# Reversing the column order of the single-pass matmuls in a hybrid decoder block

## The chip, the cores and the metric

The kernel runs on one core of a Trainium2 chip. The metric is device time in microseconds, the median of several runs of the whole program. A profile of one execution gives each instruction of the core's engines: TensorE (PE, and PEld for its weight loads), VectorE (DVE), ScalarE (ACT), GpSimd (POOL), and SyncE (SP), which issues DMA transfers.

## The reference

One layer of a decoder block over 512 tokens of width 1024, in float32:

```python
h = rms_norm(x, norm_mix_pre)
proj = h @ w_in                      # q, k, v, gates of both mixers
o_gla = gla_mixer(...)               # chunked gated linear attention, 4 heads
o_nsa = nsa_mixer(...)               # compressed + selected + window attention, 8 heads
mixed = (sigmoid(merge_gla) * (o_gla @ w_proj_gla)
         + sigmoid(merge_nsa) * (o_nsa @ w_proj_nsa))
x = x + rms_norm(mixed @ w_out, norm_mix_post)
h = rms_norm(x, norm_ffn_pre)
f = (silu(h @ w_ffn_gate) * (h @ w_ffn_up)) @ w_ffn_down     # inner width 2816
x = x + rms_norm(f, norm_ffn_post)
```

Nearly all of the arithmetic is in the dense products with weights.

## The kernel before

A matmul on TensorE loads a weight tile of up to 128 x 128 (the stationary operand) and then streams the columns of a moving operand past it; the results, column by column, go to one bank of PSUM (128 partitions x 512 float32 columns), where they replace what is there or are added to it.

**Single-pass products.** Float32 operands that need full precision are split into two tiles of type float32r, a rounded high part and the rest: `xh`, `xl` for activations, `wh`, `wl` for weights. A product is then three matmuls that add up in PSUM: `wh` with `xh`, `wh` with `xl`, `wl` with `xh`. A float32r matmul reads its columns once, and is called single-pass here. The others work on plain float32 and have two records each in the profile: the transposes with `ident`, the inner products of the linear attention (L585 to L636), the compression (L836) and the compressed scores (L886).

**Where the single-pass products are**, in the order of the program:

- the token-major part of `w_in` (L463 to L465): 3 groups of 440 columns, over 4 token blocks and 8 blocks of the model width;
- `prod` (L174 to L176), used by `dense_h` and others: 128 output features by all 512 tokens (or half of them), over the model width in steps of 128;
- `eproduct` (L383): pairs of weight tiles of `w_in` in a seven-product scheme on halves (256 columns), with sums of activations and weights formed beforehand (`EF`, `eform`);
- the gates of the linear attention (L519), 512 columns;
- the attention: scores (`part` in `scores`, L970 and L971, widths 128 to 512), the start of a head (L1010) and the weighted values (`add` in `values`, L1034 to L1037, widths 512 down to 128);
- `ffn_half` (L1258 to L1260): the first feed-forward blocks, 256 columns;
- `product` in `unit` (L1416): 19 feed-forward blocks in the same seven-product scheme, 256 columns, 84 matmuls each;
- `down_product` (L1706): the down projection in that scheme, 256 columns, 147 matmuls per pair of output blocks.

All their operands have columns that lie next to each other in memory. Among the float32 matmuls, `compress` reads its moving operand with a step of 16 floats:

```python
blocks = ct.rearrange("p b (n s) -> p b n s", s=16)
pe.matmul(ps[:, 0:130].rearrange("p (b n) -> p b n", b=2), cw1[:, p, :], blocks[:, :, o:o + 65, w], ...)
```

**Order of the work.** The tile framework takes the instructions in the order in which the kernel's code issues them to the five engines (with a few marked to be issued after others) and puts semaphores where a tile is written by one engine and read by another. `Stream` loads weights on SP's queue some tiles ahead; ScalarE makes the high part, and VectorE, or an adding DMA of POOL's queue, the low part. PSUM has four tags of two banks each (`mm`, `sc`, `tp`, `acc`); VectorE and ScalarE read a bank when the last matmul of its group has ended.

Of the kernel before, what the change touches and what calls it, by code (L numbers as in the profile page):

```python
# [18 lines left out]
KD = D // 128  # L19
# [73 lines left out]
def hybrid_block_kernel(ctx: ExitStack, tc: tile.TileContext, I, outT):  # L93
# [4 lines left out]
    wts = ctx.enter_context(tc.tile_pool(name="wts", bufs=1, side="right"))  # L98
    psum = ctx.enter_context(tc.tile_pool(name="psum", bufs=1, space=PSUM))

    def bank(tag):
        return psum.tile([128, 512], F32, tag=tag, bufs=2, name="ps_" + tag)

# [63 lines left out]
    def prod(ps, w, xh, xl, k0, kn, ktot, t=ALL):  # L167

        wh, wl = w
        marks = []  # L170
        for kk in range(kn):
            k = k0 + kk
            c = slice(kk * 128, (kk + 1) * 128)
            pe.matmul(ps[:, t], wh[:, c], xh(k)[:, t], start=(k == 0), stop=False)  # L174
            pe.matmul(ps[:, t], wh[:, c], xl(k)[:, t], start=False, stop=False)  # L175
            marks.append(pe.matmul(ps[:, t], wl[:, c], xh(k)[:, t], start=False, stop=(k == ktot - 1)))  # L176
        return marks

    def hh(k):
# [188 lines left out]
    def eproduct(u, i):  # L368
        a, b = USE[i]
        if a == "a11":  # L370
            p = [bank("mm"), bank("mm")]
            ebank[u] = p if u % 2 == 0 else p[::-1]
            eus[u] = gt.tile([128, 2, 256], F32, tag="eus", bufs=1, name="eus")
        p1, p2 = ebank[u]
        r1, rb, r2, ra = p1[:, 0:256], p1[:, 256:512], p2[:, 0:256], p2[:, 256:512]
        u2, u3 = eus[u][:, 0, :], eus[u][:, 1, :]
        o, first = {"a11": (r1, True), "s2": (r2, True), "s3": (rb, False), "s1": (ra, False), "a12": (r1, False),
                    "a22": (rb, False), "s4": (ra, False)}[a]
        (wh, wl), (xh, xl) = ew.pop((u, a)), EF[b]
        for q in range(4):  # L380
            c = slice(q * 128, (q + 1) * 128)
            for m, (w, x) in enumerate(((wh, xh), (wh, xl), (wl, xh))):
                pe.matmul(o, w[:, c], x[q], start=(first and q == 0 and m == 0), stop=(q == 3 and m == 2),  # L383
                          skip_group_check=True)

        def add(out, y):
            return dve.tensor_tensor(out=out, in0=o, in1=y, op=OP.add)  # L387

        if a == "a11":
            out_of[u, a] = act.copy(u2, o)  # L390
        elif a == "s2":
            add(u2, u2)
        elif a == "s3":
            out_of[u, a] = add(u3, u2)
        else:
            if u not in edst:
                edst[u] = [early_dest(n) for n in EPAIRS[u]]
            d0, d1 = edst[u]
            if a == "s1":
                add(d1[:, halves[1]], u3)  # L400
            elif a == "a22":
                add(d1[:, halves[0]], u2)
            elif a == "s4":
                out_of[u] = add(d0[:, halves[1]], u2)
            else:
                act.copy(d0[:, halves[0]], o)
                for n in EPAIRS[u]:
                    if T_R <= n < T_MA:
                        proj_r(n - T_R)
# [40 lines left out]
    for g in range(3):  # L450
        pss = [bank(t) for t in tags[g]]
        for c in range(4):
            wh, wl = st.next(("tok", g, c))
            for i in range(NT):
                if (g, c, i) == (0, 3, 2):
                    ps = token_sums([acc_x], "acc")
                    rsqrt_mean(rs_x, ps[:, 0:NT], D, EPS)
                t = slice(i * 128, (i + 1) * 128)
                for kk in range(2):
                    k = 2 * c + kk  # L460
                    w = slice(kk * TG, (kk + 1) * TG)
                    o = pss[i][:, 0:TG]
                    pe.matmul(o, hu[:, k, t], wh[:, w], start=(k == 0), stop=False)  # L463
                    pe.matmul(o, hul[:, k, t], wh[:, w], start=False, stop=False)
                    pe.matmul(o, hu[:, k, t], wl[:, w], start=False, stop=(k == KD - 1))  # L465
            if g > 0:
                beside.pop(0)()
        if g == 0:
            ps = over_partitions(rs_x, "acc")
            act.copy(rb_x, ps)  # L470
        for i in range(NT):
            c0, c1 = g * TG, (g + 1) * TG
            if c0 < 1024:
                act.activation(out=tok[i][:, c0:min(c1, 1024)], in_=pss[i][:, 0:min(c1, 1024) - c0], func=AF.Copy,
                               scale=rs_x[:, i:i + 1])
            if c1 > 1024:
                act.activation(out=tokb[:, i, 0:c1 - 1024], in_=pss[i][:, 1024 - c0:TG], func=AF.Copy,
                               scale=rs_x[:, i:i + 1])
# [34 lines left out]
    def gates_two(h0):  # L513
        aT, w3 = stk["a"], stk["w"]
        for h in (h0, h0 + 1):
            low = gt.tile([128, S], F32, tag=("e2", "dd", "sr", "sr")[h],
                          bufs=(1, 2, 4, 4)[h], name="low")
            ps = bank("sc")
            pe.matmul(ps, w3[:, h * 128:(h + 1) * 128], aT, start=True, stop=True)  # L519
            stk["abs"] = act.activation(out=lam[:, h], in_=ps, func=AF.Abs, bias=b_alpha[:, h:h + 1])  # L520
            dve.tensor_scalar(out=low, in0=ps, scalar1=b_alpha[:, h:h + 1], scalar2=0.0,
                              op0=OP.add, op1=OP.min)
            lows.append(low)
# [431 lines left out]
    def scores(h, b):  # L955
# [7 lines left out]
        def part(blks, last):  # L963
            ps = bank("sc")
            col = 0
            for i in blks:
                n = 128 * (i + 1)
                s = ps[:, col:col + n]
                t = slice(i * 128, (i + 1) * 128)
                pe.matmul(s, q1[:, t], ka[b][:, 0:n], start=True, stop=False)  # L970
                pe.matmul(s, q3[0:66, t], kb[b][0:66, 0:n], start=False, stop=True)  # L971
                col += n
            col = 0
            for i in blks:
                n = 128 * (i + 1)
                s = ps[:, col:col + n]
                o = p[:, OFF[i]:OFF[i] + n]
                dve.tensor_tensor_reduce(out=o, in0=s, in1=causal[:, S - n:S], scale=-1.0, scalar=-NEG,  # L978
                                         op0=OP.add, op1=OP.min, accum_out=mx[:, i:i + 1])
                act.activation(out=o, in_=o, func=AF.Exp, scale=-1.0, bias=mx[:, i:i + 1],  # L980
                               accum_out=z[:, i:i + 1])
                col += n
            if last:
                dve.reciprocal(z, z)
                dve.tensor_tensor(out=z, in0=z, in1=gates[:, :, 3 * h + (1 if b == "s" else 2)], op=OP.mult)
                for i in range(NT):
                    n = 128 * (i + 1)
                    o = p[:, OFF[i]:OFF[i] + n]
                    dve.tensor_scalar(out=o, in0=o, scalar1=z[:, i:i + 1], scalar2=None, op0=OP.mult)  # L989
# [17 lines left out]
    def head_start(h):  # L1007
        ps = bank("acc")
        accs[h] = ps
        pe.matmul(ps, vc3[:, h // 4, :], c3s.pop(h), start=True, stop=False)  # L1010

    def values(h, b):
        p = units.pop((h, b))
# [15 lines left out]
        def add(k):  # L1029
# [1 line left out]
            r = slice(k * 128, S)  # L1031
            end = b == "w" and k == NT - 1
            if not end:
                pe.matmul(ps[:, r], vv[b][:, k, :], ph[:, r], start=False, stop=False)  # L1034
            pe.matmul(ps[0:64, r], vv[b][:, k, 0:64], pl[:, r], start=False, stop=False)
            if end:
                pe.matmul(ps[:, r], vv[b][:, k, :], ph[:, r], start=False, stop=True)  # L1037

        return turn, add

# [207 lines left out]
    def ffn_half(e, w, ps, ks=range(KD)):  # L1248
# [3 lines left out]
        for k in ks:  # L1252
            i, j = k // 2, k % 2
            c = slice(k * 128, (k + 1) * 128)
            for x in range(2):
                wh, wl = w[x]
                o = ps[x][:, t]
                pe.matmul(o, wh[:, c], h2h[i][:, j, t], start=(k == 0), stop=False)  # L1258
                pe.matmul(o, wh[:, c], h2l[i][:, j, t], start=False, stop=False)
                last = pe.matmul(o, wl[:, c], h2h[i][:, j, t], start=False, stop=(k == KD - 1))  # L1260
            marks.append(last)
        return marks

# [141 lines left out]
    def unit(n, between=None):  # L1405
# [5 lines left out]
        def product(o, a, b, first):  # L1411
            (ah_, al_), (bh_, bl_) = forms.pop((n, a)), XF[b]
            for q in range(4):
                c = slice(q * 128, (q + 1) * 128)
                for i, (w, x) in enumerate(((ah_, bh_), (ah_, bl_), (al_, bh_))):
                    pe.matmul(o, w[:, c], x[q], start=(first and q == 0 and i == 0), stop=(q == 3 and i == 2),  # L1416
                              skip_group_check=True)

        def add(out, ps, b):
# [269 lines left out]
    def down_product(j):  # L1689
# [13 lines left out]
        for q in range(KH):  # L1703
            c = slice(q * 128, (q + 1) * 128)
            for i, (w, x) in enumerate(((wh, xh), (wh, xl), (wl, xh))):
                pe.matmul(o, w[:, c], x[q], start=(first and q == 0 and i == 0), stop=(q == KH - 1 and i == 2),  # L1706
                          skip_group_check=True)
        if a == "a11":
            act.copy(u2, r1)
# [143 lines left out]
```

## Time and profile before

| | |
|---|---|
| median of 3 runs | 864.79 us (864.34 to 865.26) |
| span of the profiled execution, first to last instruction | 862.0 us (its time as a run is not listed apart from the span) |
| mean granted TensorE clock | 0.996 |
| TensorE busy | 845.4 us, 98% |
| weight loads busy | 769.0 us, 89% |
| VectorE, ScalarE, GpSimd busy | 635.0, 530.2, 141.4 us |
| TensorE's share of the chain that ended last | 85% |

Matmuls are pipelined and their ends are modelled: a matmul's row is longer than the distance to the next one's start. The time of a stream of matmuls is therefore read from starts, or from the chain, in which each piece begins where the one before ended. A group of instructions is a line of the kernel with its engine, operation, tiles (out<-in) and shape; behind the bar stand its busy time, the mean of one in ns, and the idle time before. An instruction inside a helper has the helper's line.

### The profile page before, as it was taken

The page shows a single profiled execution, that of the slowest core. Times are in us where ns is not written, and L with a number is a line of the kernel's source. Part 1 is how long each engine was busy: PE and PEld are TensorE (multiplying, and loading weights), DVE is VectorE, ACT ScalarE, POOL GpSimd, SP SyncE. Part 2 cuts the span into 40 slices and gives each one's busy share as a digit, 9 for nine tenths or more (in the row PEclk, how much of TensorE's full clock was granted, in tenths as well). Part 3 has the DMA queues.
Part 4 walks back from the last instruction along what each step waited for, and adds up shares of the span by engine and source line. Part 5 has one row for each costly group of instructions (what it writes and reads, how often), then busy time and mean ns, then how long its engine had stood idle before and what let it go on. Part 6 is the DMA issues. An engine that isn't in the chain of part 4 may idle for free.

```text
span 862.0 us, 14708 instructions
## 1 busy us (share of the span) xinstructions
PE 845.4 (98%) x5592; PEld 769.0 (89%) x5592; DVE 635.0 (74%) x1206; ACT 530.2 (62%) x964; POOL 141.4 (16%) x170
## 2 busy tenths in 40 slices
PE   9999899999999999999999999999999999999995
PEld 8998799998888788888887999899999999889995
DVE  7766897873375778877666478997778779829886
ACT  7458667663453888888634587666666557525441
POOL 1001122221020100010000354111111110001353
PEclk9999999999999999999999999999999999999998
DMA  8433455763241454545227769679787772335322
GB/s 284 108 94 113 111 102 132 156 139 90 73 154 50 97 115 108 123 98 122 62 75 260 215 171 252 124 183 239 171 179 191 194 170 75 95 89 171 86 99 98
DMA packets 41095, 117.86 MB, mean 137 GB/s; under 512 B 4700, under 2 KB 6764, under 8 KB 40896
## 3 DMA queue, kind: packets, MB, share of 16 engines
q1 hardware_dynamic: 27808, 82.49, 30.6%
q0 software_dynamic: 12496, 33.88, 21.4%
q8 instruction: 44, 0.72, 0.3%
q10 hardware_dynamic: 720, 0.54, 0.2%
q14 instruction: 27, 0.22, 0.1%
HBM read 102.21 MB, written 4.19 MB: 123 GB/s over the span
## 4 chain that ended last, share of the span: by engine, by line
PE 85%; DVE 4%; ACT 4%; issue 3%; DMA 2%; POOL 1%; SPq 0%; DVEq 0%; ACTq 0%; POOLq 0%
PE ps_mm L174 6%; PE ps_mm L176 6%; PE ps_mm L175 6%; PE ps_mm L383 6%; PE ps_mm L1416 6%; PE ps_tp L1416 6%; PE ps_sc L1416 6%; PE ps_acc L1416 5%; PE ps_sc L1706 4%; PE ps_acc L1706 2%; PE ps_mm L1706 2%; PE ps_tp L1020 2%; PE ps_acc L174 1%; PE ps_acc L175 1%; PE ps_acc L176 1%
## 5 line engine op out<-in xcount | busy, mean ns | idle before, releaser
L59 ACT CAST whi<-wraw 128x1024 fp32r<-128x1024 f32 (+2 forms) x63 | 61.1, 971 | 66.8 <-PE ps_mm L175 17.1
L174 PE MATMUL ps_mm<-hT_hi,whi 128*128 128x512 f32 x200 | 82.0, 410 | 0.0
L65 DVE TENSOR_TENSOR wlo<-wraw,whi 128x1024 fp32r<-128x1024 f32 (+2 forms) x48 | 53.4, 1113 | 36.5 <-ACT whi L59 34.0
L175 PE MATMUL ps_mm<-hT_lo,whi 128*128 128x512 f32 x200 | 79.4, 397 | 0.0
L176 PE MATMUL ps_mm<-hT_hi,wlo 128*128 128x512 f32 x200 | 79.2, 396 | 0.0
L176 PEld LDWEIGHTS ps_mm<-hT_hi,wlo 128*128 128x128 f32 x200 | 37.7, 188 | 9.0 <-DVE wlo L65 0.3
L174 PEld LDWEIGHTS ps_mm<-hT_hi,whi 128*128 128x128 f32 x200 | 37.8, 189 | 7.9
L175 PEld LDWEIGHTS ps_mm<-hT_lo,whi 128*128 128x128 f32 x200 | 37.9, 189 | 6.6
L192 DVE TENSOR_TENSOR pl<-ps_tp,ph 128x512 fp32r<-128x512 f32 (+1 forms) x64 | 31.1, 489 | 14.5 <-ACT ph L191 13.9
L980 ACT ACTIVATE p<-p,mx 128x512 f32<-128x512 f32 (+1 forms) x64 | 35.9, 560 | 9.0 <-DVE mx L978 8.0
L978 DVE CUSTOM_DVE_ANT_0 p<-ps_sc,causal 128x512 f32<-128x512 f32 (+1 forms) x64 | 30.2, 486 | 11.2 <-PE ps_sc L971 10.9
L63 POOL DMA_DIRECT2D wlo<-wraw x15 | 12.7, 849 | 155.3 <-ACT wlo L62 90.6
L1315 POOL DMA_DIRECT2D w_uu<-in_w_up x19 | 16.2, 855 | 86.3 <-PE ps_sc L1416 27.0
L191 ACT CAST ph<-ps_tp 128x512 fp32r<-128x512 f32 (+1 forms) x64 | 26.4, 415 | 4.4 <-PE ps_tp L1020 3.9
L383 PE MATMUL ps_mm<-hT_hi,feq 128*128 128x256 f32 x144 | 26.5, 280 | 2.6 <-DVE gq L387 2.5
L1020 PE MATMUL ps_tp<-ident,p 128*128 128x128 f32 x160 | 27.9, 273 | 0.0
L1020 PEld LDWEIGHTS ps_tp<-ident,p 128*128 128x128 f32 x160 | 20.8, 140 | 7.2 <-ACT pc L913 0.3
L383 PEld LDWEIGHTS ps_mm<-hT_hi,feq 128*128 128x128 f32 x144 | 22.5, 188 | 3.0 <-DVE gq L387 2.7
L1331 ACT CAST w_hl<-s 128x1024 fp32r<-128x1024 f32 x12 | 12.6, 1048 | 19.6 <-issue 15.8
L1331 ACT CAST w_d1h<-s 128x1024 fp32r<-128x1024 f32 x13 | 13.7, 1052 | 17.2 <-issue 12.5
L1331 ACT CAST w_d0h<-s 128x1024 fp32r<-128x1024 f32 x13 | 13.7, 1050 | 16.7 <-issue 12.5
L989 DVE TENSOR_SCALAR p<-p,z 128x128 f32<-128x128 f32 (+1 forms) x64 | 20.4, 382 | 0.4
(954 smaller groups left out, 3249.9 us busy)
## 6 DMA issues: line engine op xcount, KB each, us to landing
wraw<-in_w_t SPq DMA_DIRECT2D x36, 512.0 KB, 3.9
wraw<-in_w_gate SPq DMA_DIRECT2D x21, 512.0 KB, 5.9
rw<-in_w_up SPq DMA_DIRECT2D x19, 512.0 KB, 4.2
wlo<-wraw POOLq DMA_DIRECT2D x15, 512.0 KB, 4.5
wlo<-in_w_gate POOLq DMA_DIRECT2D x13, 512.0 KB, 7.3
wraw<-in_w_tok SPq DMA_DIRECT2D x12, 440.0 KB, 4.1
w_uu<-in_w_up POOLq DMA_DIRECT2D x19, 256.0 KB, 5.9
wraw<-in_w_proj SPq DMA_DIRECT2D x8, 512.0 KB, 3.5
```

The costliest lines, as they stand in the source:

```text
L59: self.nc.scalar.copy(hi[:, :cols], raw[:, :cols])
L65: self.nc.vector.tensor_tensor(out=lo[:, :cols], in0=raw[:, :cols], in1=hi[:, :cols].bitcast(F32), op=OP.subtract)
L174: pe.matmul(ps[:, t], wh[:, c], xh(k)[:, t], start=(k == 0), stop=False)
L175: pe.matmul(ps[:, t], wh[:, c], xl(k)[:, t], start=False, stop=False)
L176: marks.append(pe.matmul(ps[:, t], wl[:, c], xh(k)[:, t], start=False, stop=(k == ktot - 1)))
L192: dve.tensor_tensor(out=lo, in0=src, in1=hi.bitcast(F32), op=OP.subtract)
L383: pe.matmul(o, w[:, c], x[q], start=(first and q == 0 and m == 0), stop=(q == 3 and m == 2), skip_group_check=True)
L980: act.activation(out=o, in_=o, func=AF.Exp, scale=-1.0, bias=mx[:, i:i + 1], accum_out=z[:, i:i + 1])
L1020: pe.transpose(tp[:, i * 128:(i + 1) * 128], p[:, OFF[i] + k * 128:OFF[i] + (k + 1) * 128], ident)
L1331: act.copy(hi, t)
L1416: pe.matmul(o, w[:, c], x[q], start=(first and q == 0 and i == 0), stop=(q == 3 and i == 2), skip_group_check=True)
L1706: pe.matmul(o, w[:, c], x[q], start=(first and q == 0 and i == 0), stop=(q == KH - 1 and i == 2), skip_group_check=True)
```

## The change

A helper `mm` reverses the columns of the moving operand and of the output, and all single-pass products go through it. The weights, the numbers, the tiles, the flags and the order of all instructions stay as they were.

```diff
+    def mm(out, w, x, **kw):
+        return pe.matmul(out[:, ::-1], w, x[:, ::-1], **kw)
...
-            pe.matmul(ps[:, t], wh[:, c], xh(k)[:, t], start=(k == 0), stop=False)
-            pe.matmul(ps[:, t], wh[:, c], xl(k)[:, t], start=False, stop=False)
-            marks.append(pe.matmul(ps[:, t], wl[:, c], xh(k)[:, t], start=False, stop=(k == ktot - 1)))
+            mm(ps[:, t], wh[:, c], xh(k)[:, t], start=(k == 0), stop=False)
+            mm(ps[:, t], wh[:, c], xl(k)[:, t], start=False, stop=False)
+            marks.append(mm(ps[:, t], wl[:, c], xh(k)[:, t], start=False, stop=(k == ktot - 1)))
...
-                pe.matmul(o, hu[:, k, t], wh[:, w], start=(k == 0), stop=False)
+                mm(o, hu[:, k, t], wh[:, w], start=(k == 0), stop=False)
...
-                pe.matmul(s, q1[:, t], ka[b][:, 0:n], start=True, stop=False)
+                mm(s, q1[:, t], ka[b][:, 0:n], start=True, stop=False)
...
-                pe.matmul(ps[:, r], vv[b][:, k, :], ph[:, r], start=False, stop=False)
+                mm(ps[:, r], vv[b][:, k, :], ph[:, r], start=False, stop=False)
...
-                    pe.matmul(o, w[:, c], x[q], start=(first and q == 0 and i == 0), stop=(q == 3 and i == 2),
+                    mm(o, w[:, c], x[q], start=(first and q == 0 and i == 0), stop=(q == 3 and i == 2),
```

The same replacement stands at L383, L519, L1010, L1258 to L1260 and L1706. The helper stands three lines long ahead of the rest, so the line numbers behind it are higher by 3 in the changed kernel, and every single-pass matmul has the line of `mm`, L102.

More of the change, by code (lines that the diff above doesn't have):

```diff
@@ L382, in eproduct @@
             for m, (w, x) in enumerate(((wh, xh), (wh, xl), (wl, xh))):
-                pe.matmul(o, w[:, c], x[q], start=(first and q == 0 and m == 0), stop=(q == 3 and m == 2),
+                mm(o, w[:, c], x[q], start=(first and q == 0 and m == 0), stop=(q == 3 and m == 2),
                           skip_group_check=True)
@@ L462, in hybrid_block_kernel @@
                     o = pss[i][:, 0:TG]
-                    pe.matmul(o, hu[:, k, t], wh[:, w], start=(k == 0), stop=False)
-                    pe.matmul(o, hul[:, k, t], wh[:, w], start=False, stop=False)
-                    pe.matmul(o, hu[:, k, t], wl[:, w], start=False, stop=(k == KD - 1))
+                    mm(o, hu[:, k, t], wh[:, w], start=(k == 0), stop=False)
+                    mm(o, hul[:, k, t], wh[:, w], start=False, stop=False)
+                    mm(o, hu[:, k, t], wl[:, w], start=False, stop=(k == KD - 1))
             if g > 0:
@@ L518, in gates_two @@
             ps = bank("sc")
-            pe.matmul(ps, w3[:, h * 128:(h + 1) * 128], aT, start=True, stop=True)
+            mm(ps, w3[:, h * 128:(h + 1) * 128], aT, start=True, stop=True)
             stk["abs"] = act.activation(out=lam[:, h], in_=ps, func=AF.Abs, bias=b_alpha[:, h:h + 1])
@@ L969, in part @@
                 t = slice(i * 128, (i + 1) * 128)
-                pe.matmul(s, q1[:, t], ka[b][:, 0:n], start=True, stop=False)
-                pe.matmul(s, q3[0:66, t], kb[b][0:66, 0:n], start=False, stop=True)
+                mm(s, q1[:, t], ka[b][:, 0:n], start=True, stop=False)
+                mm(s, q3[0:66, t], kb[b][0:66, 0:n], start=False, stop=True)
                 col += n
@@ L1009, in head_start @@
         accs[h] = ps
-        pe.matmul(ps, vc3[:, h // 4, :], c3s.pop(h), start=True, stop=False)
+        mm(ps, vc3[:, h // 4, :], c3s.pop(h), start=True, stop=False)
     def values(h, b):
@@ L1033, in add @@
             if not end:
-                pe.matmul(ps[:, r], vv[b][:, k, :], ph[:, r], start=False, stop=False)
-            pe.matmul(ps[0:64, r], vv[b][:, k, 0:64], pl[:, r], start=False, stop=False)
+                mm(ps[:, r], vv[b][:, k, :], ph[:, r], start=False, stop=False)
+            mm(ps[0:64, r], vv[b][:, k, 0:64], pl[:, r], start=False, stop=False)
             if end:
-                pe.matmul(ps[:, r], vv[b][:, k, :], ph[:, r], start=False, stop=True)
+                mm(ps[:, r], vv[b][:, k, :], ph[:, r], start=False, stop=True)
         return turn, add
@@ L1257, in ffn_half @@
                 o = ps[x][:, t]
-                pe.matmul(o, wh[:, c], h2h[i][:, j, t], start=(k == 0), stop=False)
-                pe.matmul(o, wh[:, c], h2l[i][:, j, t], start=False, stop=False)
-                last = pe.matmul(o, wl[:, c], h2h[i][:, j, t], start=False, stop=(k == KD - 1))
+                mm(o, wh[:, c], h2h[i][:, j, t], start=(k == 0), stop=False)
+                mm(o, wh[:, c], h2l[i][:, j, t], start=False, stop=False)
+                last = mm(o, wl[:, c], h2h[i][:, j, t], start=False, stop=(k == KD - 1))
             marks.append(last)
@@ L1705, in down_product @@
             for i, (w, x) in enumerate(((wh, xh), (wh, xl), (wl, xh))):
-                pe.matmul(o, w[:, c], x[q], start=(first and q == 0 and i == 0), stop=(q == KH - 1 and i == 2),
+                mm(o, w[:, c], x[q], start=(first and q == 0 and i == 0), stop=(q == KH - 1 and i == 2),
                           skip_group_check=True)
```

## The prediction

> **What bounds the kernel now.** I read the page's busy shares first, then the chain that ended last, then stretches of the span, and last single matmuls in order of time.
>
> ```profile
> span 862.0 us, 14708 instructions
> PE 845.4 (98%) x5592; PEld 769.0 (89%) x5592; DVE 635.0 (74%) x1206; ACT 530.2 (62%) x964; POOL 141.4 (16%) x170
> PE 85%; DVE 4%; ACT 4%; issue 3%; DMA 2%; POOL 1%; SPq 0%; DVEq 0%; ACTq 0%; POOLq 0%
> ```
>
> TensorE is the bound: 85% of the chain that ended last is matmul time, and the other engines have slack over the span (DVE 74%, ACT 62%). The chain's remaining 15%, some 129 us, are waits for something else; they bound how much a slower TensorE could hide. The stretches say the same from another side (columns: microseconds of the stretch, busy time and count of each engine, granted clock, DMA share, GB/s):
>
> ```profile
> 300.00:505.00 205.00, 204.68 (x1150) 172.49 (x1149) 142.71 (x353) 145.17 (x302) 22.63 (x26) 1.00 0.51 136
> 560.00:735.00 175.00, 175.00 (x1476) 174.60 (x1476) 143.79 (x254) 110.78 (x170) 26.43 (x31) 1.00 0.72 173
> ```
>
> From 560 to 735 us TensorE does one thing: products of 256 columns, 1476 in 175.00 us, so 118.6 ns from start to start. The clock is at 1.00. A row's own duration (280 ns) is longer than that pitch, because neighbouring matmuls overlap; only starts can be added up. The other widths, each from starts in order of time (start, duration, what):
>
> ```profile
> 100.06 0.40 PE L174 MATMUL ps_mm<-hT_hi,whi 128*128 128x512 f32 x1
> ...
> 102.63 0.39 PE L176 MATMUL ps_mm<-hT_hi,wlo 128*128 128x512 f32 x1
> 59.82 0.36 PE L463 MATMUL ps_tp<-whi,hu_hi 128*128 128x440 f32 x1
> ...
> 62.82 0.36 PE L463 MATMUL ps_sc<-whi,hu_hi 128*128 128x440 f32 x1
> 304.06 0.34 PE L1034 MATMUL ps_acc<-ph,vvw 128*128 128x384 f32 x1
> 304.23 0.34 PE L1035 MATMUL ps_acc<-pl,vvw 128*64 128x384 f32 x1
> 304.41 0.39 PE L174 MATMUL ps_mm<-gh,whi 128*128 128x512 f32 x1
> ```
>
> 512 columns: 11 steps in 2.57 us, 233.6 ns. 440 columns: 15 steps in 3.00 us, 200.0 ns. 384 columns: two in 0.35 us, 175 ns. That is 0.456 ns per column.
>
> **The change, part by part.** Nothing is removed, added or moved. On all five engines the same instructions stand in the same order with the same tiles; only their line is now that of the helper `mm`. What differs is inside 5056 matmuls: the moving operand and the PSUM output both step by minus one column instead of plus one. Both are reversed, so column j of the input still lands in column j of the output. Weights are read as before. The fp32 matmuls (transposes, L585 to L636, L836, L886) keep their direction.
>
> The 5056, counted from the loops: 3436 of 256 columns (240 at L174 to L176, 756 at L383, 192 at L1258, 1596 at L1416, 588 at L1706, 64 in attention); 1204 of 512 (1128 at L174 to L176, 76 in attention and gates); 288 of 440; 64 of 384; 64 of 128. Present price on TensorE: 3436 x 118.6 + 1204 x 233.6 + 288 x 200.0 + 64 x 175 = 407.5 + 281.3 + 57.6 + 11.2 = 757.6 us of the 862.0, nearly all on the path. So a loss of 1% of the column rate would be 7.6 us. The step that decides is therefore one number: what a column costs when its neighbour is read and written in falling order. No row shows a falling operand, so I bound it.
>
> *The upper end* is a row in which neighbouring columns are not neighbours in memory. L836 (`compress`) reads its moving operand with a step of 16 floats. L604 is the contiguous partner, L886 a small one; all are fp32 (three rows of the chain: start, time, what; then their groups: count, busy us and mean ns, idle before):
>
> ```profile
> 255.49 7.08 PE ps_sc L836 x32
> 128.88 0.86 PE ps_sc L604 x4
> 266.33 3.79 PE ps_sc L886 x32
> L836 PE MATMUL ps_sc<-ct,cw 128*128 128x130 f32 x32 | 7.2, 398 | 0.0
> L604 PE MATMUL ps_sc<-tok,gkut 128*128 128x256 f32 x24 | 6.8, 390 | 0.0
> L886 PE MATMUL ps_sc<-kdg,qst 128*128 128x64 f32 x32 | 3.8, 277 | 0.0
> ```
>
> L836 has 16 matmuls in the program and 32 records; 221 ns per record of 130 columns is 1.70 ns per column. L604 takes 215 ns per record of 256 columns, 0.84 ns per column. Scattered reading thus costs 2.02 times. A floor under short records is no explanation, since 64 columns at L886 need only 118.4 ns. 0.84 against 0.456 for a single-pass column says that an fp32 record makes about two passes, so a scattered column costs 1.70 / 2 = 0.85 ns per pass (an estimate from these rows) where an adjacent one costs 0.42 to 0.456.
>
> *The lower end* is below nothing. L604's pass runs at 0.42 ns per column and the single-pass ones at 0.456, so something takes 18.6 ns from each matmul of 512 (233.6 against 215). A narrow weight takes away part of it:
>
> ```profile
> 302.45 0.39 PE L1034 MATMUL ps_acc<-ph,vvw 128*128 128x512 f32 x1
> 302.68 0.39 PE L1035 MATMUL ps_acc<-pl,vvw 128*64 128x512 f32 x1
> 302.90 0.40 PE L174 MATMUL ps_mm<-ga,whi 128*128 128x512 f32 x1
> ```
>
> After L1035 the next matmul starts 0.22 us later, after L1034 0.23. So weight load and moving stream may meet somewhere, and another order of columns might meet differently.
>
> *The value I take is no change of the column price.* Falling unit steps are nearest to the contiguous rows: as in L604 the next column is the neighbouring word, and as in L836 it is not. If a fetch brings neighbours together and serves what is asked of them, the direction does not matter: the pair (511, 510) lies in the same place as (510, 511), the widths 256, 384, 440 and 512 are even, and their start offsets are even too, so that pairs stay whole. Both ends stay for the range.
>
> The Trainium skill speaks to this in two places that pull apart. Its page PSUM — Partial Sum Buffer, section Specifications (TRN2), says of the 8-byte cachelines that "any non-contiguous AP slows matmuls significantly"; if a falling step counts as non-contiguous, the time would be that of the slow rival below. Its page Advanced Engine Details and Errata, section SBUF Cachelines, says that accesses to the same 16-byte line run at full performance and that a line needs at least two hits; by that a falling step has as many hits as a rising one and the sum is zero. The trace agrees with the second for L836, whose step of 64 bytes has one hit per line and runs at half rate; no run here shows a PSUM output that is not contiguous.
>
> *What follows on the other engines.* Readers of PSUM wait for the matmul that ends a group, not for a column, so they start where they did. The 256-column products have a small cushion: 118.6 ns is also what L886's 64 columns take (118.4), so there the weight load may be what ends last, and a few ns of slower columns would not show. The 512s have none: 1204 x 1 ns = 1.2 us for each nanosecond. If the columns stay as they are, no stall goes and none comes. Sum: 862.0 + 0 in the profiled execution's span; the three runs before have a median of 864.79, 2.8 us above that span, so 864.8 us.
>
> **The rivals.** *Half rate (ends slower).* The place is the moving read or the PSUM write of each single-pass matmul. The mechanism: two neighbours are joined in one access only when the second follows the first upward. For it: L836 proves that TensorE loses half its rate as soon as neighbours are not joined. Against it: L836's neighbours cannot be joined in any order. Price, at 0.851 ns per column: 512 columns 436 ns (+202), 440: 374 (+174), 384: 327 (+152), 256: 218 (+99), 128 stay. 1204 x 202 + 288 x 174 + 64 x 152 + 3436 x 99 = 243 + 50 + 10 + 340 = 643 us, so 1508; some of the chain's 129 us of waits would hide behind the longer matmuls, at most to about 1400. It decides once a 256-column matmul passes its 118.6 ns.
>
> *A part of it (slower).* A falling stream loses a slot only now and then, say when it crosses into a new stretch that a rising one would have fetched ahead. A quarter of the full loss is 161 us (1026), half of it 322 (1187); a few ns on the 512s alone give 867 to 880. For it: the single-pass columns already lose 0.036 ns each somewhere, so that path has no slack. Against it: no row shows which part.
>
> *Faster.* The 18.6 ns per 512-column matmul come from a meeting of weight load and moving stream that falling order avoids. At best 1204 x 18.6 + 288 x 15.2 + 64 x 13.7 = 27.7 us, so 837; half of it gives 851. Against it: the weights of a matmul lie in another tile than its moving operand, and nothing in the rows ties the loss to direction.
>
> *The change does nothing at all*, since both steps are turned round again before they reach the engine, ends at 864.8 too and is counted with the forecast.
>
> **How the numbers follow.** No change 0.60; half rate 0.20; a part of it 0.13; faster 0.07. Most weight goes to no change because L836 needs only lost neighbourhood, not a direction; the half rate keeps a fifth because nothing in the trace shows a falling step at all. The likeliest case's own range is 863 to 866.5, which is the spread of the runs and 0.2% (1.7 us, about what a measurement of this kernel tells from no change). The range given holds no change, the partial loss up to its half (1187) and the gain nearly to its end (840), together 0.80; the half rate at 1400 to 1508 is left out. Faster by over 0.2%: 0.07. Within 0.2%: 0.60. Slower by over 0.2%: 0.20 + 0.13 = 0.33.
>
> **What would show it.** In the stretch that now runs 560 to 735, the pitch of 256 columns is the test of the write and read together: 118.6 ns right, about 218 half rate. Starts of 512-column matmuls at 100 us: 233.6 ns right, 436 half rate, 215 the gain. L836's successor keeps 7.08 us in every case, being unchanged. If 512 and 256 stretch by the same time per column, the cost is per column; if 512 alone, the weight load covers the rest. The prediction is wrong if any of these pitches moves by over 1%, or if the pitches stand and TensorE's idle time grows.

## The result and the profile after

The changed kernel takes 869.61 us in the median of four runs (868.87 to 871.54), the kernel before 865.02 (864.34 to 865.58) beside it: a ratio of 1.0052 [1.0036, 1.0069], 4.6 us or 0.5% slower. The forecast was no change, 863 to 866.5 us in its likeliest case. The profiled execution is the slowest of the four, 871.54 us with a span of 869.6. Its page, busy shares and the split of the chain that ended last:

```profile
span 869.6 us, 14712 instructions
PE 850.8 (98%) x5592; PEld 772.8 (89%) x5592; DVE 634.9 (73%) x1206; ACT 530.5 (61%) x964; POOL 140.4 (16%) x170
PE 84%; ACT 5%; DVE 4%; issue 3%; DMA 3%; POOL 1%; SPq 0%; ACTq 0%; DVEq 0%; POOLq 0%
```

TensorE has the same 5592 records and is busy 5.4 us longer, its weight loads 3.8 us; the busy times of VectorE, ScalarE and GpSimd move by 1.0 us at most. The two stretches of the prediction (same columns as there) hold a few matmuls fewer:

```profile
300.00:505.00 205.00, 204.25 (x1129) 170.71 (x1128) 140.68 (x347) 143.96 (x297) 21.94 (x25) 1.00 0.51 135
560.00:735.00 175.00, 173.47 (x1456) 172.47 (x1455) 143.38 (x251) 108.27 (x164) 26.49 (x31) 1.00 0.74 178
```

Part of that is only a later start: a stretch of fixed times holds other work once the kernel is behind. Single matmuls and pieces of the chain say more (start, duration, what; the first two rows are single matmuls of 512 columns):

```profile
99.84 0.40 PE L102 MATMUL ps_mm<-hT_lo,whi 128*128 128x512 f32 x1
...
102.64 0.40 PE L102 MATMUL ps_mm<-hT_lo,whi 128*128 128x512 f32 x1
11.33 2.41 PE ps_mm L102 x12
257.43 7.10 PE ps_sc L839 x32
599.30 10.00 PE ps_sc L102 x84
788.99 5.98 DMA wraw<-in_w_down
807.73 5.72 DMA wraw<-in_w_down
```

512 columns: 12 steps in 2.80 us, 233.3 ns (forecast 233.6). 440: 2.41 / 12 = 201 ns (200.0). The unchanged `compress` (L836 before, L839 now): 7.10 us (7.08). 256 columns in `product`: 10.00 / 84 = 119.0 ns (118.6). None of these runs at half rate. The last two rows are pieces in which the chain now waits for loads of `w_down`.

Pairing all 5592 records of the two traces by their order shows where the 7.4 us between their last matmuls arise. Two jumps of 1.9 and 0.5 us stand at these loads. The next three executions of the changed kernel had spans of 868.1, 867.3 and 867.0, shorter by 1.5 to 2.6 us, so most of that waiting seems to belong to this execution. Another 1.2 us arise between 85 and 100 us, where this profile has a stretch of half clock that the profile of before does not have (the same window before, then after, then two single matmuls after):

```profile
88.50:91.90 3.40, 3.32 (x26) 3.19 (x26) 3.40 (x6) 0.70 (x1) 0.38 (x1) 1.00 0.79 252
```

```profile
88.50:91.90 3.40, 2.82 (x13) 2.82 (x14) 3.12 (x5) 0.20 (x1) 0.86 (x1) 0.50 0.86 249
89.46 0.42 PE L102 MATMUL ps_mm<-hT_lo,feq 128*128 128x256 f32 x1
...
91.38 0.41 PE L102 MATMUL ps_mm<-hT_lo,feq 128*128 128x256 f32 x1
```

Nine steps of 256 columns take 1.92 us there, 213 ns each, at a granted clock of 0.50. The 3.8 us that are left are small differences at many matmuls, and they show best where the prediction did not look: in `eproduct` (L383, now L102), also 256 columns, at a granted clock of 1.00 in both profiles. The same ten matmuls before, then after, first and last:

```profile
113.17 0.28 PE L383 MATMUL ps_mm<-hT_hi,whi 128*128 128x256 f32 x1
...
114.19 0.28 PE L383 MATMUL ps_mm<-hT_hi,whi 128*128 128x256 f32 x1
```

```profile
114.63 0.28 PE L102 MATMUL ps_mm<-hT_hi,whi 128*128 128x256 f32 x1
...
115.69 0.28 PE L102 MATMUL ps_mm<-hT_hi,whi 128*128 128x256 f32 x1
```

Nine steps take 1.02 us before and 1.06 after: 113.3 ns and 117.8. So the 256-column products before did not all have the pitch of 118.6 ns, and the fast ones lost their lead.

### The profile page after: what moved, and what is told of

It reads as the page before. It is cut to its first block, busy times and chain, and to the rows that moved or that the text cites. A ratio compares the mean times of both kernels' runs of the same rounds, so it can differ in the third digit from the quotient of the medians.

```text
span 869.6 us, 14712 instructions
## 1 busy us (share of the span) xinstructions
PE 850.8 (98%) x5592; PEld 772.8 (89%) x5592; DVE 634.9 (73%) x1206; ACT 530.5 (61%) x964; POOL 140.4 (16%) x170
## 4 chain that ended last, share of the span: by engine, by line
PE 84%; ACT 5%; DVE 4%; issue 3%; DMA 3%; POOL 1%; SPq 0%; ACTq 0%; DVEq 0%; POOLq 0%
PE ps_mm L102 36%; PE ps_sc L102 16%; PE ps_acc L102 14%; PE ps_tp L102 10%; PE ps_tp L1023 2%; DMA wraw<-in_w_down 1%; PE ps_sc L839 1%; PE ps_acc L623 1%; DMA wlo<-wraw 1%; PE ps_sc L607 1%; DVE wlo L195 1%; PE ps_tp L589 1%; PE ps_tp L202 0%; ACT whi L59 0%; ACT lam L533 0%
## 5 line engine op out<-in xcount | busy, mean ns | idle before, releaser
L102 PE MATMUL ps_mm<-hT_hi,whi 128*128 128x512 f32 (+1 forms) x268 | 100.1, 379 | 1.8 <-DVE y L1687 1.8
L102 PE MATMUL ps_mm<-hT_lo,whi 128*128 128x512 f32 (+1 forms) x264 | 96.7, 371 | 0.0
L102 PE MATMUL ps_mm<-hT_hi,wlo 128*128 128x512 f32 (+1 forms) x260 | 96.6, 371 | 0.0
L102 PEld LDWEIGHTS ps_mm<-hT_hi,whi 128*128 128x128 f32 x268 | 50.0, 189 | 10.2 <-ACT whi L194 1.9
L102 PEld LDWEIGHTS ps_mm<-hT_hi,wlo 128*128 128x128 f32 x260 | 48.9, 188 | 9.2 <-DVE wlo L65 0.3
L102 PEld LDWEIGHTS ps_mm<-hT_lo,whi 128*128 128x128 f32 x264 | 49.4, 189 | 6.9
L102 PE MATMUL ps_mm<-hT_hi,feq 128*128 128x256 f32 x144 | 28.6, 293 | 2.6 <-DVE gq L390 2.5
L102 PEld LDWEIGHTS ps_mm<-hT_hi,feq 128*128 128x128 f32 x144 | 23.7, 196 | 3.1 <-DVE gq L390 2.8
```

Source lines behind the costliest of these rows:

```text
L102: return pe.matmul(out[:, ::-1], w, x[:, ::-1], **kw)
```

## Experiments

Three theories were open. A: a falling operand costs something by itself, on the read of the moving columns or on the write to PSUM. B: chance in the transfers, as in the waits for `w_down` above. C: TensorE's granted clock is lower (0.992 to 0.994 in the runs of the changed kernel, 0.996 in the profile of before). A fourth, D, came from the sorting by address further down. The edits below are in `mm` unless they show other lines.

**The control.** `mm` passes both operands on as they are.

```diff
-        return pe.matmul(out[:, ::-1], w, x[:, ::-1], **kw)
+        return pe.matmul(out, w, x, **kw)
```

> The helper alone, with both operands in rising order again: a control. Theory A (falling order itself costs a little on each single-pass matmul: between the two profiles the start-to-start time grew by 0.9 ns per 256-column, 0.5 per 512-column and 1.25 per 440-column matmul, 4.1 us in all): back to before, 864.5 to 865.7 us, ratio 1.000 within 0.0015. Theory B (chance in the transfers: in the profiled run 2.5 us of extra waits stood at the w_down loads): no tie to direction, so this kernel may as well end at 867 to 870. Theory C (a lower granted clock, 0.992 to 0.994 against 0.996, makes the difference): 865 us if the clock is at 0.996, 869 if it is at 0.993, whatever the direction.

Measured: 866.04 us against 865.75, ratio 1.0007 [0.9996, 1.0019]. The helper itself costs nothing that can be told. Its trace, paired with that of before, still differs by 2.2 us (1.35 of them in a stretch of half clock, 88.6 to 92.0 us), so a difference of one trace from one other is no better than that; times below are medians of runs.

**Read alone, write alone.** The read falls and the output rises, or the other way; results are left in the wrong columns.

```diff
+        return pe.matmul(out, w, x[:, ::-1], **kw)      # read alone
+        return pe.matmul(out[:, ::-1], w, x, **kw)      # write alone
```

> Only the moving operand is read in falling order; PSUM is written in rising order, so the columns of each product come out reversed and the output is not the reference's. Theory A with the price on the read: 869 to 870 us, ratio 1.004 to 1.006, the 256-column pitch about 0.6 to 0.9 ns over before. Theory A with the price on the write: 864.5 to 865.7. Theory B: no prediction by direction, anything from 865 to 870. Theory C: goes with the granted clock alone.

> Only PSUM is written in falling order; the moving operand is read in rising order, so the columns of each product come out reversed and the output is not the reference's. Theory A with the price on the write: 869 to 870 us. Theory A with the price on the read: 864.5 to 865.7. If each side has a part, about 867 here and in the run with the read alone. Theory C: goes with the granted clock alone.

Measured: read alone 869.07 us, 1.0039 [1.0027, 1.0051]; write alone 865.65, 1.0004 [0.9995, 1.0012]. The same ten matmuls of `eproduct`, read alone and then write alone:

```profile
114.43 0.28 PE L102 MATMUL ps_mm<-hT_hi,whi 128*128 128x256 f32 x1
...
115.49 0.28 PE L102 MATMUL ps_mm<-hT_hi,whi 128*128 128x256 f32 x1
```

```profile
115.69 0.28 PE L102 MATMUL ps_mm<-hT_hi,whi 128*128 128x256 f32 x1
...
116.71 0.28 PE L102 MATMUL ps_mm<-hT_hi,whi 128*128 128x256 f32 x1
```

117.8 ns and 113.3 ns. The price is on the read; a PSUM output written backwards costs nothing that can be told. Theory B falls with these runs: the kernels that rise on the read stay at the time of before, the one that falls does not. The write-alone kernel also shows what theory C is worth. Its profiled execution had a lower mean clock than any run of the changed kernel (core, span, clock):

```profile
core 0: 866.2 us, clock 0.990
```

and yet these matmuls have their old pitch. The mean is lower because two stretches, 88.1 to 94.9 and 562.5 to 566.0 us, run at 0.50; elsewhere, from 7 us on to the last matmul, the clock is at 1.00, and the profile of before has no such stretch between 6 us and its last matmul. So the clock does not set the pitches that are compared here, but it moves the time of a run: one such stretch of 3.4 us cost 1.2 us in the changed kernel and 1.35 in the control. The runs with the read alone had clocks of 0.991 to 0.994, and a part of their 3.3 us goes with that. At equal clocks a loss stays: runs at 0.994 have a mean of 868.1 us with the read alone (2 runs only) and 865.8 in the kernel before on the same chip (10 runs).

**Only products of up to 256 columns fall**; wider ones keep their direction.

```diff
     def mm(out, w, x, **kw):
+        if x.shape[1] > 256:
+            return pe.matmul(out, w, x, **kw)
         return pe.matmul(out[:, ::-1], w, x[:, ::-1], **kw)
```

> Both operands fall in the matmuls of up to 256 columns (3500 of 5056) and rise in those of 384, 440 and 512. Theory A by the small per-matmul differences of the two profiles: 3.2 of the 4.2 us remain, 868.2 us. A price per column alone (4.3 us over 1.66 million columns) would leave 53% of it, 867.3 us. Theories B and C: 865 or 869.6 with no tie to the widths.

Measured: 868.38 us, 1.0031 [1.0019, 1.0043]. Most of the loss is in the 256s, which the prediction had called cushioned.

**Sorting by address.** The addresses of the tiles follow from the sizes and the order in which the kernel asks for them. For each 256-column matmul I took the byte address at which the next matmul's weights start, less the one at which its own moving columns start, modulo 128, and grouped the pitches (start to start, in ns, count in brackets; steps with a wait or half clock in them left out). For the falling kernel the address is that of the same tile, though its last column is read first.

| difference | before | write alone | after | read alone |
|---|---|---|---|---|
| 0 | 118.8 (505) | 118.8 | 118.3 | 118.3 |
| 32 | 118.6 (1225) | 118.6 | 117.8 | 117.8 |
| 64 | 115.6 (1397) | 115.6 | 118.0 | 118.0 |
| 96 | 118.0 (170) | 118.2 | 117.9 | 118.0 |
| all | 117.3 | 117.4 | 118.0 | 118.0 |

In rising order one class of four is 3 ns faster; in falling order the classes are alike, near 118. That is theory D: what counts is how weights and moving columns lie to each other, and the falling order loses the good case. In the changed kernel the class at 64 loses 1397 x 2.4 ns = 3.4 us, and the class at 32 gives 1.0 us back. It can be tried without any falling column: move the tiles. Two limits of the sorting: by the address of a matmul's own weights the pitches of before sort as well as by that of the next ones, so which of the two counts is not shown; and the four classes hold only a quarter of the variance of the pitches.

**Place and anti.** Both rise. Spacers of 64 bytes and tiles made wider bring the difference to 64 for 3014 of 3409 neighbours (1418 before) in the one ("place"), and to 0 for all in the other ("anti"). The core of the edit against the control, and what the second does otherwise:

```diff
-    rs_x = base.tile([128, NT], F32, name="rs_x")
+    rs_x = base.tile([128, 32], F32, name="rs_x")[:, 0:NT]
...
+                pad_k.append(mid.tile([128, 16], F32, name="pad_k"))
...
+            pad.append(ffn.tile([128, 16], F32, name="pad_e"))
...
+    pad_c = ffn.tile([128, 16], F32, name="pad_c")
...
-    rs2 = ffn.tile([128, NT], F32, name="rs2")
+    rs2 = ffn.tile([128, 16], F32, name="rs2")[:, 0:NT]
```

```diff
-                pad_k.append(mid.tile([128, 16], F32, name="pad_k"))
...
+    wts.tile([128, 16], F32, name="pad_w")
...
-            pad.append(ffn.tile([128, 16], F32, name="pad_e"))
...
-    pad_c = ffn.tile([128, 16], F32, name="pad_c")
...
-    rs2 = ffn.tile([128, 16], F32, name="rs2")[:, 0:NT]
+    rs2 = ffn.tile([128, 32], F32, name="rs2")[:, 0:NT]
```

> All columns rise; spacers of 32 to 96 bytes shift tiles so that in 3014 of 3409 neighbouring 256-column matmuls the start address of the next weights minus that of the moving operand is 64 modulo 128 (1418 before), in the rest 0. Theory D (the price of falling order is a lost advantage of address: in the trace of before a 256-column matmul takes 115.6 ns where that difference is 64, and 118.0 to 118.8 where it is 0, 32 or 96; falling, it takes about 118 wherever the tiles lie): 4.7 us faster than before, ratio 0.993 to 0.996. Theory A (falling order has a price of its own, addresses do not matter): as before, ratio 1.000.

> All columns rise; spacers shift the tiles so that the difference of addresses is 0 modulo 128 for all 256-column matmuls. Theory D: 1418 matmuls lose 3.2 ns, the others stay within 1 ns, ratio 1.004 to 1.006, the 256-column pitch at 118.8 ns, without a single falling column. Theory A: as before, ratio 1.000.

Measured: place 863.7 us against 866.02, 0.998 [0.997, 0.999]; anti 868.13, 1.0036 [1.0024, 1.0048]. The ten matmuls, place and then anti:

```profile
116.30 0.28 PE L102 MATMUL ps_mm<-hT_hi,whi 128*128 128x256 f32 x1
...
117.32 0.28 PE L102 MATMUL ps_mm<-hT_hi,whi 128*128 128x256 f32 x1
```

```profile
114.48 0.28 PE L102 MATMUL ps_mm<-hT_hi,whi 128*128 128x256 f32 x1
...
115.56 0.28 PE L102 MATMUL ps_mm<-hT_hi,whi 128*128 128x256 f32 x1
96.75 0.39 PE L102 MATMUL ps_mm<-hT_hi,whi 128*128 128x512 f32 x1
...
103.78 0.39 PE L102 MATMUL ps_mm<-hT_lo,whi 128*128 128x512 f32 x1
```

113.3 ns in place, 120.0 in anti. So addresses alone move the kernel by 4.4 us, from 863.7 to 868.13, and a loss about as large as that of the read alone (1.0039) comes without a single falling column. That addresses do not matter, which theory A was taken to imply, is out. Place brought the right sign but less than the 4.7 us expected: its 256s have a mean of 116.7 ns, since in `product` the class at 64 has 117.1 and not 115.6. The trace of before had 116.7 in that class of `product` already, and 114.1 in `eproduct`, so its mean of 115.6 was no price for every place: something besides the difference modulo 128 counts. Anti held something unexpected in its last two rows: 512 columns at 31 steps in 7.03 us, 226.8 ns against 233.6. For the wide ones the difference of 0 seems to be the good one, though sorting them within a kernel hardly shows it: 232.8 ns at 0 and 233.0 at 64 before, 231.8 and 232.7 in place.

**Place, and falling.**

```diff
+        return pe.matmul(out[:, ::-1], w, x[:, ::-1], **kw)      # in place's layout
```

> The spacers of the kernel with difference 64, with columns falling as in the changed kernel. Theory D: falling order takes about 118 ns wherever the tiles lie, so the spacers give nothing and the ratio to before stays at 1.003 to 1.006. Theory A: also as the changed kernel, 1.005. If the addresses help falling columns too, 0.998 to 1.000.

Measured: 869.85 us, 1.0048 [1.0035, 1.0061]; 256 columns 118.5 ns at a difference of 64 and 118.8 at 0. In falling order the layout that was good in rising order gains nothing.

**Both good layouts.** Place, with the tiles of weights for 512-column products moved 64 bytes on, so that those have 0 (952 of 1089) and the 256s keep 64. To make room, the warm-up matmuls use another tile.

```diff
-                hi = self.pool.tile([128, 1024], F32R, tag="whi", bufs=2, name="whi")
+                at = 16 if key[0] in ("h", "pa", "pb", "o", "d") else 0
+                hi = self.pool.tile([128, 1056], F32R, tag="whi", bufs=2, name="whi")[:, at:at + 1024]
...
```

> All columns rise. As the kernel with spacers for difference 64 in the 256-column matmuls, and the tiles whi and wlo are 128 bytes wider, so that products of 512 columns use them 64 bytes further on: their difference of addresses is then 0 modulo 128 in 952 of 1089 cases (36 before), since the kernel with 0 everywhere showed 228.5 ns for 512 columns from hT where before shows 233. Theory D: 256 columns at 116.7 ns as with the first spacers (2 us less than before), 512 columns near 229 (4 us less): ratio 0.991 to 0.995. If the 512s gained there by something else than the difference: as with the first spacers, 0.998.

Measured: 863.18 us against 865.37, 0.9979 [0.997, 0.9988]: the fastest kernel of all, but no better than place within the intervals, and short of the 0.991 to 0.995 expected. Its 512s have a mean of 231.0 ns, where 229 was expected (232.6 in place). The ratio is the one that was expected if the 512s of anti had gained by something else than the difference, so that 0 is their good case is not shown.

How far the pitches account for the times: the mean pitch of each width, less that of before, times its count in the program (3436 of 256 columns, 1204 of 512, 288 of 440), against the measured ratio and its interval times the median of before. The pitches of a row are from one profiled execution; waits and stretches of half clock are left out.

| kernel | 256 | 512 | 440 | sum of the pitches, us | measured, us |
|---|---|---|---|---|---|
| before | 117.32 | 233.02 | 200.0 | | |
| after | 117.97 | 233.53 | 201.2 | +3.2 | +4.5 (3.1 to 6.0) |
| 256s alone | 117.97 | 233.25 | 200.0 | +2.5 | +2.7 (1.6 to 3.7) |
| anti | 119.32 | 229.33 | 200.8 | +2.7 | +3.1 (2.1 to 4.2) |
| place, falling | 118.54 | 233.54 | 201.0 | +5.1 | +4.2 (3.0 to 5.3) |
| place | 116.70 | 232.62 | 200.8 | -2.4 | -1.7 (-2.6 to -0.9) |
| place, both layouts | 116.80 | 231.01 | 200.7 | -4.0 | -1.8 (-2.6 to -1.0) |

All sums lie within the measured intervals but the last, where 2 us that the pitches gave came back elsewhere; where was not settled.

**What makes a read slow.** The prediction's half rate rested on neighbours that are no neighbours in memory. Four kernels vary the pattern; x is read, or out written, in two halves that are interleaved in memory: by single columns, by pairs, by fours. The other operand of each matmul is taken as it lies, so the results are left in other columns.

```diff
+ x.rearrange("p (n f) -> p f n", f=2)                       # read in single columns, two apart
+ x.rearrange("p (n f two) -> p f n two", f=2, two=2)        # read in pairs, four apart
+ out.rearrange("p (n f two) -> p f n two", f=2, two=2)      # write in pairs, four apart, x as it lies
+ x.rearrange("p (n f four) -> p f n four", f=2, four=4)     # read in fours, eight apart
```

> The moving operand is read with a step of two columns (first the even ones, then the odd ones), PSUM is written in rising order, so the columns of each product come out permuted and the output is not the reference's. No two columns that follow each other are neighbours in memory. If TensorE needs neighbours to keep its rate (the half-rate rival of the prediction): 0.85 ns per column, 1400 to 1510 us. If it only needs some of the words of one stretch of memory to be asked for soon after each other: 865 to 875 us.

> The moving operand is read in pairs of neighbouring columns, the pairs four columns apart (0,1,4,5,... and then 2,3,6,7,...), PSUM is written in rising order; the columns come out permuted, so the output is not the reference's. If two neighbours are all that an access joins: within 1% of before, 860 to 875 us. If an access serves a longer stretch of neighbours: between that and the 1565 us of the step of two columns.

> PSUM is written in pairs of neighbouring columns, the pairs four columns apart, and the moving operand is read in rising order; the columns come out permuted, so the output is not the reference's. If pairs are all that a write joins: as before, 863 to 868 us. If any output that is not contiguous slows a matmul: 1200 us or more.

> The moving operand is read in fours of neighbouring columns (16 bytes), the fours eight columns apart (0 to 3, 8 to 11, ... and then 4 to 7, 12 to 15, ...); PSUM is written in rising order, the columns come out permuted, so the output is not the reference's. If an access brings four neighbouring words and takes about 1.75 ns (228.2 ns for the 128 accesses of 256 columns read in twos, 117 for the 64 of 256 in fours): within 1% of before, 862 to 872 us. If any pattern with gaps halves the rate, whatever lies between them: about 1560 us.

Measured: single columns 1565.06 us, 1.8083 [1.8052, 1.8114]; pairs 1564.38, 1.8084 [1.8051, 1.8117]; fours 867.28, 1.0018 [1.0008, 1.0029]; pairs on the write 864.89, 1.0 [0.9988, 1.0013]. Single columns, two single matmuls and a piece of the chain; the same piece with pairs; one with fours:

```profile
179.76 0.65 PE L102 MATMUL ps_mm<-hT_hi,whi 128*128 128x512 f32 x1
...
182.94 0.65 PE L102 MATMUL ps_mm<-hT_lo,whi 128*128 128x512 f32 x1
...
1058.54 19.17 PE ps_sc L102 x84
```

```profile
1058.30 19.17 PE ps_sc L102 x84
```

```profile
598.05 10.00 PE ps_sc L102 x84
```

84 matmuls of 256 columns take 19.17 us, 228.2 ns each, with single columns and with pairs alike, and 10.00 us (119.0) with fours. Seven steps of 512 columns take 3.18 us, 454 ns. This fits a price for each visit of the stream to a piece of 16 bytes: single columns two apart and pairs four apart both take two words of the four at a time, and two that are neighbours are no better than two with a gap. Between the two widths, 128 more such pieces cost 454 - 228.2 = 226 ns, 1.76 ns each, and L836 in the prediction, with one column in each piece, took 1.70 ns per column. A falling step uses all four words of a piece, in the other order. The fours, which rise, are 0.18% slower than before all the same, and their 256 columns take 118.1 ns at a difference of 64: they lost the good case too, so it is not the falling direction alone that loses it. By the same price a contiguous matmul of 256 columns needs 64 x 1.76 + 3 = 116 ns for its pieces alone (an estimate; the 3 ns are what 128 pieces leave of 228.2). The pitches of 113.3 to 120.0 lie around that, so it is no floor to the nanosecond, but it suggests that single-pass products run near the limit of the moving read, where a meeting worth a few ns is not covered by anything. No run shows that limit by itself.

## Why the prediction was off by half a per cent

The range that was given, 840 to 1187 us, holds the measured time, but it is wide enough to hold the better part of two rivals as well. The likeliest case, 863 to 866.5, was missed.

**The bound.** Right: TensorE's stream sets the time, 84% of the chain. TensorE's idle time in the profile grew from 16.6 to 18.8 us; most of that seems to belong to the one execution that was profiled.

**"The value I take is no change of the column price."** This is the step that failed, by a little. There is no price per column: 512 columns lost 0.5 ns and 256 lost 0.65 in the mean, and the classes lost between -0.8 and +2.4. The argument, that a fetch serves what is asked of it in either direction, held for the rate: both falling and rising read every piece once, and the half rate did not come. It put at nothing what the prediction itself had suspected, that weights and moving stream meet and that another order of columns might meet differently. The 757.6 us of exposed matmul time made 0.4% of pitch into 3 us.

**"The 256-column products have a small cushion."** This was wrong, and here most of the loss fell. The pitch of 118.6 ns came from one stretch, 560 to 735 us, and its likeness to L886's 118.4 was taken for a floor. `eproduct`'s rows at 113 us show 113.3 ns for the same width. Ahead of the change that row would have said that 118.6 is no floor, and that something other than columns sets the pitch. It moved by 4%. The pitches that the prediction had named as its test moved by less than its 1% (118.6 to 119.0, 233.6 to 233.3), so that test looked in the wrong place.

**The rival "faster".** Its mechanism, a meeting of weight load and moving stream that depends on the order of columns, is the one the runs support best, with the sign turned round: rising order had a good case (difference 64) in two fifths of the 256s, and the falling columns show none. The objection raised against it, that weights lie in another tile than the moving operand, was mistaken: how the two tiles lie to each other moves the time. The Trainium skill's page TensorE: Matmul & The Clock Gate, section Step-by-step: what each phase is for, says that loading the next weights takes no read bandwidth from the running matmul; place against anti (863.7 and 868.13 us, addresses alone) shows that where the weights lie does matter to the running matmuls here; that it is the load of the next ones that meets them is argued, not shown.

**The rival "a part of it".** The time lies at its lower end, 867 to 880 from "a few ns on the 512s alone". The place was the 256s and the mechanism another than a stretch that a rising stream would have fetched ahead: place, falling shows the loss with a layout that makes the rising one fastest.

**The rival "half rate".** It did not come, since falling neighbours still share their 16 bytes. Its price came out close, 256 columns 218 ns and 512 columns 436 by the estimate, 228.2 and 454 measured where two words of four were taken at a time, but by luck: the estimate halved L836's 1.70 ns per column for two passes, while the price per 16-byte piece that the runs gave, 1.76 ns, is that of one whole column of L836, which has one column in each piece. A single-pass product with one word of four at a time was not tried; by that price 256 columns would take 256 x 1.76 + 3 = 454 ns (an estimate). The whole came to 1565 us where 1400 to 1508 was said; hardly any wait hid behind the longer matmuls.

**The write.** The sentence quoted from the Trainium skill's page PSUM — Partial Sum Buffer, Specifications (TRN2), that "any non-contiguous AP slows matmuls significantly", is not borne out here for two patterns: falling columns 1.0004 [0.9995, 1.0012], pairs four columns apart 1.0 [0.9988, 1.0013]. Single columns with a gap were not tried on the write. The Trainium skill's page Advanced Engine Details and Errata, SBUF Cachelines, gave the right answer on direction up to 0.4%; its two hits per 16-byte line were not enough here, since pairs run at half rate (1.8084 [1.8051, 1.8117]) and only fours at nearly the full one.

**What stays open.** Why a difference of 64 bytes is good for 256 columns, what made the 512s of anti faster, and why the falling read and the fours lose the good case, was not settled; that the two reads use the same part of the memory at the same time is a guess. Weights read in falling order were not tried. About 1.3 us of the 4.5 in the table of sums belong to no pitch there; 3.2 lies within the measured interval. One stretch of half clock more in the changed kernel's runs would be of that size (1.2 to 1.35 us), which is not shown.

## To carry to other kernels

Before a stream's pitch is called a floor, look for the same shape elsewhere in the trace: if one group runs at 113 ns and another at 119, neither is the price of its columns, and the difference is to be had or lost. Single-pass matmuls near the rate of their moving read feel where weight and moving tiles lie relative to each other, so tiles of odd small sizes in front of them are worth a spacer, a gain of 0.2% here. The step of a moving operand matters by whether four neighbouring words are used together; its direction is nearly free on the read (0.4% here, less at equal clocks), and on the write no price could be told.

## What was not expected of the hardware

- Spacers of a few dozen bytes moved this kernel between 863.7 and 868.13 us with the same instructions in the same order; 256 columns went from 116.7 to 119.3 ns and 512 columns the other way, from 232.6 to 229.3.
- Two neighbouring words of each 16 bytes are read no faster than two with a gap: 228.2 ns per 256 columns in both, 1564.38 and 1565.06 us in all.
- Among runs of one kernel the granted clock goes with the time: the kernel before took 864.8 us in the mean at 0.996 (6 runs) and 868.2 at 0.993 (3 runs) on one chip, a spread nearly as wide as the effect that was studied. In the traces a lower mean is a few stretches of 3.4 us or so at half clock, 213 ns per 256 columns, and not a slower pitch everywhere; so runs are best compared at equal clocks.
